# A decoder layer in fp32: squares and residual of the output projection added by transfers, and the MLP's first group in another order

## The chip, the cores and the metric

The kernel runs on 1 core of a Trainium2 chip. The metric is the time of one execution in device microseconds. Before the change the median of three runs is 2737.82 us (2735.27 to 2740.61).

## The reference, cut to what matters

One decoder layer over 2048 tokens of width 1024. Two groups of token-mixer heads (a gated delta rule and HGRN2) make `mix`; the lines that the change bears on come after them:

```python
mix_out = jnp.einsum('btc,cd->btd', mix, w_out[i])          # 1024 x 1024
h = h + rms_norm(mix_out, post_mix_norm[i])

u = jnp.einsum('btd,df->btf', rms_norm(h, pre_mlp_norm[i]), w_mlp_up[i])   # 1024 -> 4096
y = jnp.einsum('btf,fd->btd', jnp.square(jax.nn.relu(u)), w_mlp_down[i])
h = h + rms_norm(y, post_mlp_norm[i])
...
gate = jax.nn.sigmoid(jnp.einsum('btd,de->bte', h, w_ple_gate[i]))
return h + e * gate
```

`rms_norm` needs the sum of squares of a token over all 1024 columns, and the second norm (of `h`, before the MLP) needs it again for the sum of the first norm's result and the residual.

## The kernel before, in words

**Arithmetic.** Every large matmul is made of three: an fp32 operand is split into a high half, copied by ScalarE (ACT), and a low half, the difference, made by VectorE (DVE) (`split`, L164 and L165), and high x high, high x low and low x high are summed in PSUM. TensorE (PE) thus waits for a block until ACT and DVE have both treated it.

**Stages.** The mixers run until about 1105 us, then the output projection (tiles `mmo`, to 1316), the MLP's up projection in Strassen's form (tiles `u`: seven products of half-size blocks for each group of columns), the down projection (`d`) and the gate (`mmg`).

**Output projection.** Tokens lie in four quarters q of 512, output columns in eight blocks d of 128, and the loop runs over 32 tiles j = 8q + d; a tile is 24 matmuls (8 blocks of the inner dimension by 3). Tiles 0 and 1 are made early, among the mixers. For tile j, `stage_out` starts the load of 512 KB of weights three tiles ahead (`raw_out`, 2 buffers), `ready_out` splits it two tiles ahead into `w_out` (3 buffers). In quarter 0 the split weights are also kept in DRAM, and quarter 3 reloads them whole, 1 MB a tile (`w_out24` to `w_out31`, L185). ACT copies the finished bank to `yo` and squares it (`squares`): the first square of a quarter goes into `acc_o`, the others into a scratch tile `sq_o`, which DVE adds to `acc_o` (L228).

**Norm and residual.** At the end of a quarter `rstd_steps` makes 1/rms from `acc_o` with two matmuls against ones and some work on ACT and DVE. For quarters 0 and 1 `residual` follows: for each of eight tiles it loads `xo` from the input (SP's queue, L1139), scales `yo` (DVE, L1188), adds `xo` (DVE, L1189), squares the sum into `sq_h`/`acc_h`, and stores it to `h1d` (L1185, L1195). `early_operands` loads parts of `h1d` back (`be`), scales and splits them into the operands `t11`, `t21` of the first MLP group. Quarters 2 and 3 are only stored (`yod`) and treated later.

**What sets the order.** PE's order is written by hand and kept. Every eighth matmul calls `tick()`, which advances generators that `later(gen, offsets)` has put at given ticks; `OUT_STEPS` gives the ticks of the norm and the residual. DVE, ACT, GpSimd (POOL) and SyncE (SP, which issues nearly all transfers) each run their instructions in the order that results from it, and an instruction that waits holds what stands behind it on its engine.

**Start of the MLP.** In the last tiles of the projection the four blocks of the first up weights are loaded into two tiles `u_raw` and split. Blocks that are sums or differences ("3", "1", "2", "4") are made by DVE in place. The first group is made `together`: its last five products share their passes over the inner dimension:

```python
seven = (("11", "11"), ("12", "21"), ("2", "2"), ("3", "3"), ("22", "4"), ("1", "1"), ("4", "22"))
...
for k in range(KD // 2):
    for ps, (w, m) in zip(sums, rest):
        product(ps, columns(x[w])[k : k + 1], t[m][k : k + 1], k == 0, k == KD // 2 - 1)
```

`up_weights(0, 1)` makes the blocks `wu` of the second group: its first step loads the blocks `a` (L1381), and the rest (splits and sums) runs when the first group has been issued and the projection's buffers are closed, since the blocks' pool `bp` lies in their space.

Of the kernel before, what the change touches and what calls it, by code (L numbers as in the profile page):

```python
# [10 lines left out]
F32 = mybir.dt.float32  # L11
# [35 lines left out]
OUT_STEPS = (1, 5) + tuple(range(7, 15)) + (15, 25)  # L47
# [41 lines left out]
def trunk(ctx, tc, x, xT, pT, vecs, w_in, w_ab, gdn_a_log, gdn_dt_bias, w_out, w_up, w_down,  # L89
# [129 lines left out]

    def squares(acc, src, k, name, eng=V):  # L220

        if acc is None:
            acc = st.tile([P, QT], F32, tag="acc", name=f"acc_{name}", bufs=3)
            S.activation(acc, src, AF.Square)
        else:
            sq = st.tile([P, QT], F32, tag="sq", name=f"sq_{name}_{k}", bufs=1)
            S.activation(sq, src, AF.Square)  # L227
            eng.tensor_tensor(acc, acc, sq, ALU.add)  # L228
        return acc
# [967 lines left out]

    def normed(q, ys, acc, skip, gain, dst, name, sums=None, pool=None):

        rd = []  # L1200
        yield from rstd_steps(acc, 1.0 / D, EPS, f"{name}{q}", rd.append, pool)
        total = yield from residual(q, lambda d: ys[d], rd[0], skip, gain, dst, name, sums)
# [20 lines left out]
    def run(gen):  # L1223
        for _ in gen:
            pass
# [85 lines left out]

    for j, (q, d) in enumerate(order):
# [36 lines left out]
        acc = squares(acc, ps, d, f"o{q}")  # L1349
# [7 lines left out]
    b2 = two_blocks(("1", s1), None)  # L1357
    V.tensor_tensor(a11, s1, a11, ALU.subtract)
# [6 lines left out]
    bp = []  # L1365

    def block(name):

        return bp[0].tile([P, 2, KD // 2, P], F32R, tag="blk", name=name)
# [69 lines left out]
    def up(half, g, x, between, together=False):  # L1439
# [12 lines left out]
        for i, (w, m) in enumerate(seven):  # L1452
# [52 lines left out]
    def down_pair(half, j):  # L1505
# [5 lines left out]
        a = bp[0].tile([P, 2, QT], F32R, tag="blk", name=f"da_{half}_{j}")  # L1511
# [7 lines left out]
        b = bp[0].tile([P, 2, QT], F32R, tag="blk", name=f"db_{half}_{j}")  # L1519
# [160 lines left out]
    def embedded(q, d, rsb):  # L1680

        t = bp[0].tile([P, 2, QT], F32, tag="blk", name=f"eg{q}_{d}")
# [100 lines left out]
```

## Time and profile before

| | |
|---|---|
| median of 3 runs | 2737.82 us (2735.27 to 2740.61) |
| profiled execution, its own time | 2733.95 us |
| its span | 2732.0 us, granted PE clock 0.993 |
| PE busy | 2661.9 us, 97% |
| DVE, ACT, POOL busy | 2047.2 (75%), 1469.8 (54%), 101.5 (4%) us |
| output projection, quarters 0 to 3 | about 1133 to 1316 us |
| first MLP group | 1316 to about 1360 us |

How to read it: PE runs nearly without a break, so the time is its work plus its idle time and the matmuls that run at less than the full rate. A share of 75% for DVE is a mean over the stages; in the stretch from 1200 to 1260 us it is busy for 52.24 of 60 us.

### The profile page before, as it was taken

To read this page: it belongs to the slowest core of one execution; us is meant where nothing else is said; L and a number is where in the kernel's file an instruction comes from. 1 tells how busy PE (TensorE), PEld (TensorE's weight loads), DVE (VectorE), ACT (ScalarE), POOL (GpSimd) and SP (SyncE) were. 2 spreads that over 40 slices of the span, in tenths; PEclk is the share of its full clock that TensorE was granted. 3 is DMA by queue.
4 is the path that set the end of the run, shared out by engine and by line. 5 is a ranking of instruction groups with operands and counts; after the bars stand their busy time and mean duration, and the time that the engine had idled before them with its cause. 6 is when DMAs were issued, how large, how long until landed. Compare 5 with 4: busy or idle time off the path is not lost.

```text
span 2732.0 us, 38440 instructions
## 1 busy us (share of the span) xinstructions
PE 2661.9 (97%) x12745; PEld 2217.0 (81%) x12745; DVE 2047.2 (75%) x4244; ACT 1469.8 (54%) x2944; POOL 101.5 (4%) x104
## 2 busy tenths in 40 slices
PE   7999999999999999999899999999999999999999
PEld 5788888888888887877788888888888888888887
DVE  6788877787778777577889867767787765567776
ACT  6665554465446445576555645555454455465422
POOL 0000000000000000000000000001000000001000
PEclk9999999999999999999999999999999999999999
DMA  7777777667666665787466547667564446687663
GB/s 247 264 262 229 243 251 251 220 224 256 203 212 220 214 216 163 267 295 239 150 225 224 189 149 260 205 208 241 170 204 145 152 171 208 191 256 246 215 211 133
DMA packets 268741, 589.23 MB, mean 216 GB/s; under 512 B 55658, under 2 KB 60232, under 8 KB 249344
## 3 DMA queue, kind: packets, MB, share of 16 engines
q1 hardware_dynamic: 268544, 586.79, 64.7%
q8 instruction: 101, 1.65, 0.3%
q14 instruction: 96, 0.79, 0.1%
HBM read 419.75 MB, written 166.92 MB: 215 GB/s over the span
## 4 chain that ended last, share of the span: by engine, by line
PE 51%; DVE 3%; DMA 3%; issue 2%; ACT 2%; POOL 1%; SPq 0%; POOLq 0%; DVEq 0%; ACTq 0%
PE u L1119 22%; PE d L1119 21%; PE mmg L1119 6%; PE mmo L1119 1%; POOL acc_y L228 1%; DMA raw_out<-in_w_out_dram 1%; DMA xo<-in_xT_dram 0%; DMA b<-h1d 0%; DMA mixT<-mixd 0%; DVE t L165 0%; DMA rd_g<-m_g 0%; DVE w_out L165 0%; DMA raw_pT<-in_pT_dram 0%; DVE yo L1189 0%; ACT L1156 0%
## 5 line engine op out<-in xcount | busy, mean ns | idle before, releaser
L1048 PE MATMUL mm<-xt,w 128*128 128x512 f32 x3072 | 783.8, 400 | 1.7 <-ACT zt_zg L553 1.5
L1048 PEld LDWEIGHTS mm<-xt,w 128*128 128x128 f32 x3072 | 553.4, 189 | 102.2 <-ACT zt_zg L553 1.9
L1119 PE MATMUL d<-db,da 128*128 128x512 f32 x2688 | 610.5, 389 | 0.2 <-DVE db L218 0.2
L1119 PE MATMUL u<-t,wu 128*128 128x512 f32 x2604 | 593.2, 390 | 3.4 <-ACT wu L164 3.4
L1119 PEld LDWEIGHTS d<-db,da 128*128 128x128 f32 x2688 | 504.6, 188 | 105.5 <-DVE db L218 0.5
L1119 PEld LDWEIGHTS u<-t,wu 128*128 128x128 f32 x2604 | 489.6, 188 | 106.4 <-ACT wu L164 4.2
L218 DVE TENSOR_TENSOR db<-db 128x512 fp32r<-128x512 f32 x224 | 160.9, 718 | 68.8 <-ACT db L217 68.3
L1448 DVE TENSOR_TENSOR u<-u,u 128x512 f32<-128x512 f32 x224 | 150.5, 683 | 63.0 <-PE u L1119 61.2
L1119 PE MATMUL mmo<-mixT,w_out 128*128 128x512 f32 x720 | 170.5, 398 | 10.9 <-DVE w_out L165 6.3
L217 ACT ACTIVATE db<-db 128x512 fp32r<-128x512 f32 x224 | 140.9, 629 | 73.5 <-DMA db<-hid 69.2
L1119 PE MATMUL mmg<-h2T,wg 128*128 128x512 f32 (+1 forms) x792 | 174.7, 383 | 0.0
L1119 PEld LDWEIGHTS mmo<-mixT,w_out 128*128 128x128 f32 x720 | 138.1, 193 | 42.3 <-DVE w_out L165 8.0
L1489 ACT ACTIVATE u<-u 128x512 f32<-128x512 f32 x128 | 80.9, 632 | 167.5 <-DVE u L1448 167.0
L1119 PEld LDWEIGHTS mmg<-h2T,wg 128*128 128x128 f32 x792 | 145.5, 188 | 29.1
L165 DVE TENSOR_TENSOR da<-da 128x512 fp32r<-128x512 f32 x128 | 92.3, 721 | 83.0 <-ACT da L164 82.8
L164 ACT ACTIVATE da<-da 128x512 fp32r<-128x512 f32 x128 | 80.5, 629 | 128.1 <-DMA da<-sumd 110.4
L164 ACT ACTIVATE wu<-a 128x512 fp32r<-128x512 f32 x124 | 73.9, 622 | 50.1 <-DMA a<-in_w_up_dram 48.5
L674 DVE TENSOR_TENSOR pr_g<-xs_g,sys_g 128x16 f32<-128x16 f32 (+14 forms) x240 | 94.3, 393 | 5.6
L228 POOL TENSOR_TENSOR acc_y<-acc_y,sq_y 128x512 f32<-128x512 f32 x28 | 38.8, 1386 | 1371.6 <-ACT sq_y L227 1332.5
L165 DVE TENSOR_TENSOR wu<-a,wu 128x512 fp32r<-128x512 f32 x124 | 84.8, 688 | 3.3 <-ACT wu L164 3.2
L1490 ACT ACTIVATE u<-u 128x512 f32<-128x512 f32 x128 | 80.7, 631 | 3.7
L165 DVE TENSOR_TENSOR da<-dr,da 128x512 fp32r<-128x512 f32 x96 | 66.3, 691 | 18.2 <-ACT da L164 16.1
(383 smaller groups left out, 3792.0 us busy)
## 6 DMA issues: line engine op xcount, KB each, us to landing
w<-cache_in SPq DMA_DIRECT2D x96, 1024.0 KB
db<-hid SPq DMA_DIRECT2D x224, 256.0 KB
cache_in<-w SPq DMA_DIRECT2D x32, 1024.0 KB
hid<-u SPq DMA_DIRECT2D x128, 256.0 KB
da<-sumd SPq DMA_DIRECT2D x128, 256.0 KB
a<-in_w_up_dram SPq DMA_DIRECT2D x124, 256.0 KB
hid<-ht SPq DMA_DIRECT2D x96, 256.0 KB
dr<-in_w_down_dram SPq DMA_DIRECT2D x96, 256.0 KB
```

Of the source, the lines that this page charges most:

```text
L164: S.activation(t[:, 0], raw, AF.Copy)
L165: eng.tensor_tensor(t[:, 1], raw, t[:, 0], ALU.subtract)
L217: S.activation(t[:, 0], plain(t), AF.Copy)
L218: V.tensor_tensor(t[:, 1], plain(t), t[:, 0], ALU.subtract)
L228: eng.tensor_tensor(acc, acc, sq, ALU.add)
L674: V.tensor_tensor(pr[:, :, :, 0:i], xs[:, None, :, 0:i].broadcast_to([P, 2, GC, i]), sys[:, 0:i, i : i + 2].rearrange("p j two -> p two j" ...
L1048: PE.matmul(ps, *terms[i], start=i == 0, stop=i == nt - 1)
L1119: PE.matmul(ps, a, b, start=start, stop=stop)
L1448: V.tensor_tensor(c[new], c[old], ps, ALU.add)
L1489: S.activation(c[k], c[k], AF.Relu)
L1490: S.activation(c[k], c[k], AF.Square)
```

## The change

Six edits, of which the first four concern the output projection.

1. `squares` can add by a transfer: for tiles 1 to 6 of every quarter the sum `acc_o += sq_o` becomes a transfer issued by POOL that adds to its target (`accum_op`). Tile 7 stays with DVE.
2. `residual_by_dma` takes the place of `residual` for quarters 0 and 1: DVE scales `yo`, and a transfer from the input in DRAM adds the residual to it. The loads `xo` go. Squares and stores run three steps later, and `OUT_STEPS` has three more steps.
3. During the projection the scratch tile of a square alternates between the buffers "late" (2) and "sq" (1).
4. `early_operands` takes every second tick instead of each.
5. In the first MLP group the differences for "2" and "4" are made before the split of "3", and the five shared products run as "3" and "22" first, then "2", "1", "4".
6. Two of ten block buffers get a pool of their own (`b2`) ahead of `bp`, so that the second group's first blocks can be split during the first group's third and fourth product.

```diff
-OUT_STEPS = (1, 5) + tuple(range(7, 15)) + (15, 25)
+OUT_STEPS = (1, 5) + tuple(range(7, 18)) + (18, 26)
...
+            turns[0] += 1
+            if pair[0] and turns[0] % 2:
+                sq = st.tile([P, QT], F32, tag="late", name=f"sq_{name}_{k}")
+            else:
+                sq = st.tile([P, QT], F32, tag="sq", name=f"sq_{name}_{k}", bufs=1)
             S.activation(sq, src, AF.Square)
-            eng.tensor_tensor(acc, acc, sq, ALU.add)
+            if eng is None:
+                G.dma_start(acc, sq, accum_op=ALU.add)
+            else:
+                eng.tensor_tensor(acc, acc, sq, ALU.add)
...
+    def residual_by_dma(q, ys, rsb, skip, gain, dst, name, sums):
+
+        total, lag = None, 3
+        for d in range(KD + lag):
+            yield
+            if d < KD:
+                V.scalar_tensor_tensor(ys[d], ys[d], col(gain + d), rsb, ALU.mult, ALU.mult)
+                G.dma_start(ys[d], skip(d), accum_op=ALU.add)
+            if d >= lag:
+                total = squares(total, ys[d - lag], d - lag, f"{sums}{q}")
+                nc.sync.dma_start(dst[d - lag], ys[d - lag])
...
+            V.tensor_tensor(a11, s1, a11, ALU.subtract)
+            V.tensor_tensor(s4, s4, a11, ALU.subtract)
             u_block("3", b22, a21)
         if (q, d) == (2, 1):
             early = early_operands()
-            later(early, range(KD))
+            later(early, range(0, 2 * KD, 2))
...
-        acc = squares(acc, ps, d, f"o{q}")
+        acc = squares(acc, ps, d, f"o{q}", V if d + 1 == KD else None)
...
-    b2 = two_blocks(("1", s1), None)
-    V.tensor_tensor(a11, s1, a11, ALU.subtract)
-    u_block("2", b2, a11)
-    V.tensor_tensor(s4, s4, a11, ALU.subtract)
+    u_block("2", two_blocks(("1", s1), None), a11)
     u_block("4", wp.tile([P, 2, KD // 2, P], F32R, tag="raw", name="w_u4", bufs=2), s4)
     run(prep)
+    pair[0] = False
...
+    bp, blocks = [ctx.enter_context(tc.tile_pool(name="b2", bufs=2, reuse_waits="tile"))], [0]
...
+                for them in ((1, 2), (0, 3, 4)):
+                    for k in range(KD // 2):
+                        for r in them:
+                            w, m = rest[r]
+                            product(sums[r], columns(x[w])[k : k + 1], t[m][k : k + 1], k == 0, k == KD // 2 - 1)
...
-    up(0, 0, x, {}, True)
+    up(0, 0, x, {2: [gen], 3: [gen]}, True)
     wctx.close()
-    bp.append(ctx.enter_context(tc.tile_pool(name="bp", bufs=10, side="right", reuse_waits="tile")))
+    bp.append(ctx.enter_context(tc.tile_pool(name="bp", bufs=8, side="right", reuse_waits="tile")))
```

**How the order moves.** The names carry a running number; a first number after `yo`, `h1d`, `xo` is the quarter, the next the tile. First DVE's row in quarter 2, around the low half of `w_out22`, in the kernel before:

```order
L1189 TENSOR_TENSOR yo1_2_12656<-yo1_2_12656,xo1_2_13093 128x512
L1247 SCALAR_TENSOR_TENSOR be_3_13134<-be_3_13134,cols_87,rn0_12951 128x512
L1188 SCALAR_TENSOR_TENSOR yo1_3_12719<-yo1_3_12719,cols_87,r_o1_13021 128x512
L228 TENSOR_TENSOR acc_h1_13076<-acc_h1_13076,sq_h1_2_13131 128x512
L165 TENSOR_TENSOR t11_0_3_13137<-be_3_13134,t11_0_3_13137 128x512
L1189 TENSOR_TENSOR yo1_3_12719<-yo1_3_12719,xo1_3_13127 128x512
L1247 SCALAR_TENSOR_TENSOR be_7_13156<-be_7_13156,cols_87,rn0_12951 128x512
L1188 SCALAR_TENSOR_TENSOR yo1_4_12784<-yo1_4_12784,cols_87,r_o1_13021 128x512
L228 TENSOR_TENSOR acc_h1_13076<-acc_h1_13076,sq_h1_3_13153 128x512
L165 TENSOR_TENSOR t21_0_3_13159<-be_7_13156,t21_0_3_13159 128x512
L1189 TENSOR_TENSOR yo1_4_12784<-yo1_4_12784,xo1_4_13149 128x512
L165 TENSOR_TENSOR w_out22_13192<-raw_out22_13123,w_out22_13192 128x1024
```

The scaling (L1188), the residual add (L1189) and the add of squares (L228) of quarter 1 stand interleaved with the operands `be` and `t` of the MLP, ahead of the split. After the change, the same stretch beginning right behind the low half of `w_out21`:

```order
L1213 SCALAR_TENSOR_TENSOR yo1_3_12696<-yo1_3_12696,cols_87,r_o1_12999 128x512
L1213 SCALAR_TENSOR_TENSOR yo1_4_12757<-yo1_4_12757,cols_87,r_o1_12999 128x512
L1273 SCALAR_TENSOR_TENSOR be_2_13115<-be_2_13115,cols_87,rn0_12946 128x512
L1213 SCALAR_TENSOR_TENSOR yo1_5_12812<-yo1_5_12812,cols_87,r_o1_12999 128x512
L237 TENSOR_TENSOR acc_h1_13098<-acc_h1_13098,sq_h1_1_13111 128x512
L165 TENSOR_TENSOR t11_0_2_13118<-be_2_13115,t11_0_2_13118 128x512
L1213 SCALAR_TENSOR_TENSOR yo1_6_12862<-yo1_6_12862,cols_87,r_o1_12999 128x512
L165 TENSOR_TENSOR w_out22_13135<-raw_out22_13077,w_out22_13135 128x1024
L237 TENSOR_TENSOR acc_h1_13098<-acc_h1_13098,sq_h1_2_13143 128x512
L1273 SCALAR_TENSOR_TENSOR be_6_13161<-be_6_13161,cols_87,rn0_12946 128x512
L237 TENSOR_TENSOR acc_h1_13098<-acc_h1_13098,sq_h1_3_13157 128x512
L1213 SCALAR_TENSOR_TENSOR yo1_7_12909<-yo1_7_12909,cols_87,r_o1_12999 128x512
```

The scalings (now L1213) run ahead of the adds of squares (L237), the residual adds are gone, and the low half of `w_out22` stands eight rows behind that of `w_out21`. The add of `sq_h1_3` stands ahead of the scaling of `yo1_7`.

SP's queue before quarter 3, in the kernel before (L185 is the reload of 1 MB):

```order
L1185 DMA h1d1_2_139<-yo1_2_12656 128x512
L1139 DMA xo1_4_13149<-in_xT_dram 128x512
L1185 DMA h1d1_3_140<-yo1_3_12719 128x512
L1139 DMA xo1_5_13171<-in_xT_dram 128x512
L185 DMA w_out24_13288<-cache_out0_11786 128x2048
L1185 DMA h1d1_4_141<-yo1_4_12784 128x512
L1139 DMA xo1_6_13199<-in_xT_dram 128x512
L1352 DMA yod2_5_12206<-yo2_5_13282 128x512
L1326 DMA u_raw0_13515<-in_w_up_dram 128x512
L1185 DMA h1d1_5_142<-yo1_5_12831 128x512
```

and after:

```order
L1217 DMA h1d1_5_142<-yo1_5_12812 128x512
L1291 DMA b2_0_0_13372<-h1d1_0_137 128x512
L1381 DMA yod2_4_12205<-yo2_4_13189 128x512
L1217 DMA h1d1_6_143<-yo1_6_12862 128x512
L1291 DMA b3_0_0_13375<-h1d1_4_141 128x512
L1353 DMA u_raw0_13483<-in_w_up_dram 128x512
L1217 DMA h1d1_7_144<-yo1_7_12909 128x512
L1353 DMA u_raw1_13484<-in_w_up_dram 128x512
L185 DMA w_out24_13253<-cache_out0_11786 128x2048
L1381 DMA yod2_5_12206<-yo2_5_13247 128x512
L1353 DMA u_raw0_13483<-in_w_up_dram 128x512
```

The loads `xo` are gone, and the reload `w_out24`, which stood between the stores of `h1d1_3` and `h1d1_4`, stands behind the store of `h1d1_7` and two loads of up weights.

PE's row in the first MLP group, in the kernel before, behind the second product:

```order
L1119 MATMUL u2_0_0_13828<-t2_0_0_13466,w_u1_13772 128x512 x3
L1119 MATMUL u3_0_0_13829<-t3_0_0_13441,w_u22_13721 128x512 x3
L1119 MATMUL u22_0_0_13830<-t4_0_0_13479,w_u22_13721 128x512 x3
L1119 MATMUL u1_0_0_13831<-t1_0_0_13444,w_u1_13772 128x512 x3
L1119 MATMUL u4_0_0_13832<-t22_0_0_13482,w_u4_13779 128x512 x3
L1119 MATMUL u2_0_0_13828<-t2_0_1_13551,w_u1_13772 128x512
L1150 MATMUL nrm_o3_13849<-hl_o3_13802,ones_94 128x512
L1151 MATMUL nrm_o3_13849<-hl_o3_13802,ones_94 128x512
L1119 MATMUL u2_0_0_13828<-t2_0_1_13551,w_u1_13772 128x512 x2
```

and after:

```order
L1128 MATMUL u3_0_0_13806<-t3_0_0_13409,w_u22_13689 128x512 x3
L1128 MATMUL u22_0_0_13807<-t4_0_0_13447,w_u22_13689 128x512 x3
L1128 MATMUL u3_0_0_13806<-t3_0_1_13503,w_u22_13689 128x512 x3
L1128 MATMUL u22_0_0_13807<-t4_0_1_13541,w_u22_13689 128x512 x3
L1128 MATMUL u3_0_0_13806<-t3_0_2_13589,w_u22_13689 128x512 x3
L1128 MATMUL u22_0_0_13807<-t4_0_2_13618,w_u22_13689 128x512
L1159 MATMUL nrm_o3_13826<-hl_o3_13773,ones_94 128x512
L1160 MATMUL nrm_o3_13826<-hl_o3_13773,ones_94 128x512
L1128 MATMUL u22_0_0_13807<-t4_0_2_13618,w_u22_13689 128x512 x2
L1128 MATMUL u3_0_0_13806<-t3_0_3_13669,w_u22_13689 128x512 x3
L1128 MATMUL u22_0_0_13807<-t4_0_3_13714,w_u22_13689 128x512 x3
L1128 MATMUL u2_0_0_13805<-t2_0_0_13434,w_u1_13742 128x512 x3
```

Before, each pass takes one step of "2" (`w_u1`'s other half), "3", "22", "1" and "4" in turn; now "3" and "22" have all their passes ahead of the first step of "2", with the two matmuls of the norm `nrm_o3` among them.

More of the change, by code (lines that the diff above doesn't have):

```diff
@@ L218, in split_in_place @@
         V.tensor_tensor(t[:, 1], plain(t), t[:, 0], ALU.subtract)
+    pair, turns = [False], [0]
     def squares(acc, src, k, name, eng=V):
@@ L1196, in residual @@
         return total
+    def residual_by_dma(q, ys, rsb, skip, gain, dst, name, sums):
[8 more added lines that the diff above has]
+                nc.sync.dma_start(dst[d - lag], ys[d - lag])
+        yield
+        return total
     def normed(q, ys, acc, skip, gain, dst, name, sums=None, pool=None):
@@ L1201, in normed @@
         yield from rstd_steps(acc, 1.0 / D, EPS, f"{name}{q}", rd.append, pool)
-        total = yield from residual(q, lambda d: ys[d], rd[0], skip, gain, dst, name, sums)
+        if name == "o":
+            total = yield from residual_by_dma(q, ys, rd[0], skip, gain, dst, name, sums)
+        else:
+            total = yield from residual(q, lambda d: ys[d], rd[0], skip, gain, dst, name, sums)
         if sums is not None:
@@ L1310, in two_blocks @@
         return halves[1]
+    pair[0] = True
     for j, (q, d) in enumerate(order):
@@ L1510, in down_pair @@
         g = j % NG
-        a = bp[0].tile([P, 2, QT], F32R, tag="blk", name=f"da_{half}_{j}")
+        a = turn_block([P, 2, QT], F32R, f"da_{half}_{j}")
         if len(wn) == 2:
@@ L1518, in down_pair @@
             nc.sync.dma_start(raw, tile[:, at * QT : (at + 1) * QT])
-        b = bp[0].tile([P, 2, QT], F32R, tag="blk", name=f"db_{half}_{j}")
+        b = turn_block([P, 2, QT], F32R, f"db_{half}_{j}")
         nc.sync.dma_start(plain(b), hidd[half, hn, g])
@@ L1680, in embedded @@
     def embedded(q, d, rsb):
-        t = bp[0].tile([P, 2, QT], F32, tag="blk", name=f"eg{q}_{d}")
+        t = turn_block([P, 2, QT], F32, f"eg{q}_{d}")
         nc.sync.dma_start(t[:, 0], ed[q][d])
```

10 lines of the change are left out of this document (4 added, 6 removed).

## The prediction

> **What bounds the kernel now.** I read the busy shares first, then the waits of TensorE (PE) between 1105 and 1360 us, then PE's timeline for the same stretch, then the windows of the output projection.
>
> ```profile
> PE 2661.9 (97%) x12745; PEld 2217.0 (81%) x12745; DVE 2047.2 (75%) x4244; ACT 1469.8 (54%) x2944; POOL 101.5 (4%) x104
> PE mmo L1119 <- DVE w_out L165: 6.3, 4, 3.1
> PE u L1119 <- ACT w_u L164: 4.1, 1, 4.1
> PE u L1119 <- ACT wu L164: 3.4, 2, 2.5
> PE mmo L1119 <- ACT sq_o L227: 2.4, 1, 2.4
> PE mmo L1119 <- ACT w_out L164: 2.2, 1, 2.2
> ```
>
> PE is busy for 2661.9 of 2732.0 us: 70 us of idle time is all that any reordering can win, and a change elsewhere counts only by what PE waits for. The five rows (total us, count, longest) name the waits of the stages that the change edits: the output projection (mmo) and the first MLP group (u). The timeline shows where they are, and a second loss behind them.
>
> ```profile
> 1168.30 0.73 PE L1119 MATMUL mmo<-mixT,w_out 128*128 128x512 f32 x2 [2.20 <-ACT w_out L164]
> 1169.56 8.91 PE L1119 MATMUL mmo<-mixT,w_out 128*128 128x512 f32 x38 [0.53 <-DVE w_out L165]
> ...
> 1215.80 3.48 PE L1119 MATMUL mmo<-mixT,w_out 128*128 128x512 f32 x8 [2.43 <-ACT sq_o L227]
> ...
> 1240.87 5.73 PE L1119 MATMUL mmo<-mixT,w_out 128*128 128x512 f32 x24 [0.25 <-DVE w_out L165]
> 1248.93 7.32 PE L1119 MATMUL mmo<-mixT,w_out 128*128 128x512 f32 x24 [2.33 <-DVE w_out L165]
> 1259.40 14.13 PE L1119 MATMUL mmo<-mixT,w_out 128*128 128x512 f32 x54 [3.15 <-DVE w_out L165]
> ...
> 1281.52 34.62 PE L1119 MATMUL mmo<-mixT,w_out 128*128 128x512 f32 x152
> 1315.98 5.60 PE L1119 MATMUL u<-t,w_u 128*128 128x512 f32 x24
> 1325.70 6.75 PE L1119 MATMUL u<-t,w_u 128*128 128x512 f32 x16 [4.12 <-ACT w_u L164]
> ...
> 1343.71 6.10 PE L1119 MATMUL u<-t,wu 128*128 128x512 f32 x24 [0.82 <-ACT wu L164]
> 1352.36 7.82 PE L1119 MATMUL u<-t,wu 128*128 128x512 f32 x27 [2.54 <-ACT wu L164]
> ```
>
> Columns: start, length, count, the wait before it in brackets. The row of 152 gives the full rate: 34.62/152 = 0.2278 us a matmul, so one output tile (24 matmuls) takes 5.47 us. Rows behind a wait are slower than that: 8 took 3.48 (1.66 too long), 24 took 7.32 (1.85), 54 took 14.13 (1.83), 16 took 6.75 (3.11), 27 took 7.82 (1.67). So a wait costs itself and then some lost clock:
>
> - token quarter 0: 2.20 + 0.53 = 2.7
> - quarters 1 and 2: waits 2.43 + 0.25 + 2.33 + 3.15 = 8.2, slow matmuls 1.66 + 0.26 + 1.85 + 1.83 = 5.6, together 13.8
> - start of the MLP: waits 4.12 + 0.82 + 2.54 = 7.5, slow matmuls 3.11 + 1.67 = 4.8, together 12.3
>
> The sum, 28.8 us, is the most the change can win here.
>
> ```profile
> 1133.00:1200.00 67.00, 64.28 (x281) 52.61 (x282) 38.95 (x54) 42.22 (x67) 2.02 (x2) 1.00 0.86 297
> 1200.00:1260.00 60.00, 51.84 (x211) 41.46 (x211) 52.24 (x79) 39.38 (x59) 0.00 (x0) 0.94 0.71 231
> 1316.00:1360.00 44.00, 36.43 (x138) 28.15 (x137) 32.73 (x53) 22.84 (x38) 0.00 (x0) 0.88 0.36 118
> ```
>
> Columns: stretch, length, busy time of PE, its weight loads, VectorE (DVE), ScalarE (ACT) and GpSimd (POOL), granted clock, share of the DMA engines, GB/s. The granted clock is 0.94 and 0.88 in the stretches with waits and 1.00 in the first. By the Trainium skill ("TensorE: Matmul & The Clock Gate", Part 1) the clock falls only after an idle window of some 3.4 us; here 24 matmuls lost 1.85 us after a wait of 2.33 us, so the measurement decides, and by the page only the 4.12 wait would carry a clock price (3.1 us of the 10.4).
>
> The two middle stages differ in kind. From 1200 to 1260 DVE is busy for 52.24 of 60 us, and what PE waits for is DVE's low half of a weight tile. From 1316 to 1360 DVE is at 32.73 of 44: there the order of the program is late, not an engine.
>
> **What comes off DVE.** The change takes 24 of the 28 adds of squares and all 16 residual adds off DVE.
>
> ```profile
> L228 DVE TENSOR_TENSOR acc_o<-acc_o,sq_o x28: 682/686/693, 1134.1 to 1323.1; 128x512 f32<-128x512 f32 x28
> L1189 DVE TENSOR_TENSOR yo<-yo,xo x16: 681/684/693, 1190.0 to 1268.1; 128x512 f32<-128x512 f32 x16
> 1241.99 0.75 DVE L1188 SCALAR_TENSOR_TENSOR yo<-yo,cols,r_o 128x512 f32<-128x512 f32 x1
> 1247.65 1.22 DVE L165 TENSOR_TENSOR w_out<-raw_out,w_out 128x1024 fp32r<-128x1024 f32 x1
> 1258.13 1.22 DVE L165 TENSOR_TENSOR w_out<-raw_out,w_out 128x1024 fp32r<-128x1024 f32 x1
> ```
>
> 24 × 0.686 + 16 × 0.684 = 16.5 + 10.9 = 27.4 us of DVE work, all between 1134 and 1323. It only counts where PE waits for DVE. Between the scaling at 1241.99 and the low halves of w_out21 (1247.65) and w_out22 (1258.13) stand seven adds that go (two of squares, five of residuals; counted in DVE's timeline from the first of these rows to the last), three of them ahead of w_out21. In the new order w_out21's half stands behind three scalings and no add, so it would be done at about 1244.5, before PE finishes tile 20 at 1246.6. The three waits of 0.25, 2.33 and 3.15 go, and the wait of 2.43 (a PSUM bank held by a late square) loses its cause with the second scratch buffer. Upper bound of this term: −13.8.
>
> **What stands in its place.** Each residual tile is now a chain: scaling on DVE, an accumulating transfer issued by POOL, its landing, then the square on ACT and the store to h1d on SP. SP is in order, and the first 1 MB weight reload of quarter 3 (w_out24), which stood between the stores of h1d1_3 and h1d1_4, now stands behind all eight, h1d1_7 the last. And DVE's scaling of yo1_7 stands behind the add of sq_h1_3, which needs yo1_3's landing: two transfers in a row before the reload can be issued. No row of before has a transfer issued by POOL or one that adds; the nearest rows are loads of the same 256 KB (the first three) and of 512 KB:
>
> ```profile
> 1191.13 4.04 DMA xo<-in_xT_dram
> 1196.40 4.69 DMA xo<-in_xT_dram
> 1153.24 4.81 DMA mixT<-mixd
> 1159.71 7.45 DMA raw_out<-in_w_out_dram
> 1255.99 0.40 SPq L185 DMA_DIRECT2D w_out<-cache_out  x1
> ```
>
> I take 4.7 us for a transfer with its issue, bounded below by 4.04 and above by 2 × 4.81 = 9.6 (it reads the target before it writes it: an estimate, twice the row). With 4.7: yo1_3 scaled at 1245.4, landed 1250.1; square, add and the scaling of yo1_7 behind it, about 0.6 + 0.7 + 0.75, done 1252.2; landed 1256.9; then h1d1_7, u_raw1 and the reload issue at about 1258.5 instead of 1255.99. The reload lands between 4.8 and 7.45 us later, at 1263.3 to 1266. PE reached tile 24 at about 1259.40 + 48 matmuls = 1271.6; without its 13.8 us of loss it comes at 1257.8, and at 1260 to 1261 with what quarter 0 costs below. So a new wait of about 4 us with 2 us of slow clock behind it: −13.8 + 6 = −8 (from −13.8 at a transfer of 4.0 us and a fast reload to 0 at 7.5 us; each microsecond more delays tile 24 by two).
>
> By the Trainium skill ("DMA: Bandwidth & Descriptors", section "Anatomy of one DMA — SWDGE (gpsimd) path") such a transfer takes 2.0 us plus its bytes at 436 GB/s: 2.6 us for 256 KB, an estimate, by which the reload would be issued some 4 us sooner and this term be −12; nothing in before shows it.
>
> **Quarter 0 pays.** There DVE was not short (38.95 of 67 us), so the six adds removed win nothing, and three things are added.
>
> ```profile
> 1133.49 0.61 ACT L227 ACTIVATE sq_o<-mmo 128x512 f32<-128x512 f32 x1
> 1152.67 1.06 ACT L164 ACTIVATE w_out<-raw_out 128x1024 fp32r<-128x1024 f32 x1 [1.77 <-DMA raw_out<-in_w_out_dram]
> 1141.16 0.43 SPq L571 DMA_DIRECT2D mixd<-og_h  x1
> 1148.89 1.01 POOL L160 TENSOR_TENSOR m_g<-m_g,mhalf 128x4 f32<-128x4 f32 x1 [8.14 <-DVE m_g L274]
> q1 hardware_dynamic: 7831, 19.86, 85.4%
> ```
>
> First, the square of tile 1 (1133.49) now takes a "late" buffer, which is held until the store of og_h, issued at 1141.16, has landed; in order on ACT, the high half of w_out6 (1152.67) and PE's tile copies stand behind the squares. Second, the transfers that add into acc_o form a chain, each waiting for the one before; at 4.7 us they fit into a tile's 5.47 by 0.8. Third, POOL's m_g (1148.89), which the mixer's last normalisation and so the late weight load at 1159.71 wait for, stands behind such a transfer in POOL's order. The queue row is for 1133 to 1200: 19.86 MB with the engines busy at 85.4%. A wait of one more microsecond at two places with slow clock behind: +3.5, from 0 (all hidden under PE's 24-matmul tiles) to +10 (the engines' free 15% of 67 us filled).
>
> **Start of the MLP.** PE's first eight products' operands stand ready; at 1321.6 (1315.98 + 5.60) it wants block "2", made last.
>
> ```profile
> 1317.21 3.20 SPq L1381 DMA_DIRECT2D a<-in_w_up_dram  x4
> 1320.20 0.63 ACT L164 ACTIVATE w_u<-u_raw 128x512 fp32r<-128x512 f32 x1
> 1321.29 0.69 DVE L165 TENSOR_TENSOR w_u<-u_raw,w_u 128x512 fp32r<-128x512 f32 x1
> 1324.30 0.69 DVE L1358 TENSOR_TENSOR u_raw<-u_raw,u_raw 128x512 f32<-128x512 f32 x1
> 1325.02 0.63 ACT L164 ACTIVATE w_u<-u_raw 128x512 fp32r<-128x512 f32 x1 [0.57 <-DVE u_raw L1358]
> ```
>
> The subtraction at 1324.30 is moved ahead of the split whose low half is at 1321.29 (done 1321.98), and PE now goes through "3" and "22" first: 24 products and two of a norm, 26 × 0.2278 = 5.9 us, so block "2" is wanted at about 1327.5 where ACT began it at 1325.02 even before. The wait of 4.12 and its clock go; what remains is at most 0.4 for "3", plus the subtractions now ahead of it, 2 × 0.69. The waits of 0.82 and 2.54 for the next group's blocks go because these are split during the third and fourth product; their loads, issued from 1317.21, are there 7 us before. What moves onto ACT ahead of the norm (two splits, 2 × 0.63) I charge with 1.3: −12.3 + 1.3 = −11, from −12.3 to −5 (the norm or "4" late).
>
> **Sum.** −11 − 8 + 3.5 = −15.5; I round to −15. The profiled execution took 2733.95 (span 2732.0), 3.87 below the median 2737.82 of the three runs (2735.27 to 2740.61). So 2719 against the profiled run and **2723** on the median. A measurement here tells some 0.2% (5.5 us) from no change. The likeliest case's own range is 2710 to 2733, from its terms' ends taken together only in part.
>
> **Rivals.**
>
> - *The transfers fill the DMA engines.* For it: 85.4% in quarter 0, 0.71 from 1200 to 1260. 40 transfers of 256 KB that read and write their target are added and 16 loads dropped; quarter 0 gets the full +10 and quarters 1 and 2 give back half their gain: −11 − 6 + 12 = −5 or so, 2733. Against: the load of quarters 1 and 2 barely grows. The Trainium skill ("DMA: Bandwidth & Descriptors", section "Issuing engines are not separate DMA queues") says that queues of all engines share the same 16 DMA engines; the rows of before show one queue only, so they can't show it. Chance 0.14.
> - *Slower: the chain of transfers sets the pace.* An accumulating transfer takes longer than a tile. From 5.47 us on, the chain of acc_o holds the three scratch buffers, then ACT's squares, then PE's banks; and at 8 to 9 us the reload of w_out24 comes 2 × 4 us later than above. Quarter 0's six and quarters 1 and 2's twelve chained transfers at 3 us too much each, half of it hidden: 18 × 1.5 = +27, less 11 for the MLP: +16, 2754. For it: the 7.45 row, a chain without slack, POOL's one order for both kinds of transfer. Against: the rows of 4.0 to 4.8. It decides from about 7.5 us a transfer. Chance 0.20.
> - *The first group gains little.* Blocks are reordered, but ACT takes the new splits in a worse place (norm first, "1" and "2" behind them), or the loads behind 1317.21 land later than the third product: −5 instead of −11, 2729 to 2731. Chance 0.10.
> - The forecast: 0.56.
>
> Faster by over 0.2% (below 2732): the forecast nearly whole, 0.52, half of the third rival and a third of the first, 0.10: 0.62. Within 0.2%: 0.15. Slower: the second rival and the tail of the first, 0.23. The range takes in the whole bound of the gain less 2 below (2737.82 − 28.8 + 2 = 2711) and half of the slower rival above: 2711 to 2748.
>
> **What would show it.** Right: no wait of PE for w_out's low half between 1240 and 1262, the x16 row after u's first products at 0.228 a matmul, a wait for w_out24 of some 4 us at the start of quarter 3, small new waits in quarter 0. Wrong: accumulating transfers of over 5.5 us from issue to landing, PE waiting for ACT's sq_o or copies in quarter 0, or a wait of the first group for "3" or the norm of more than 2 us. If w_out24 doesn't wait at all, the transfers are near 2.6 us and the gain is nearer 20.

## The result: slower by 0.9%, and the profile after

| | before | changed |
|---|---|---|
| median | 2739.22 us (2735.27 to 2742.16, 4 runs) | 2765.59 us (2763.93 to 2768.14, 4 runs) |
| profiled execution's span | 2732.0 us | 2763.8 us |

The ratio is 1.0094 with a 95% interval of 1.0081 to 1.0106: slower, where faster was forecast, and above the range. The runs below were timed in groups, each with executions of the kernel before beside it (their medians lie between 2734.5 and 2739.2 us), so runs of different groups are compared by their ratios. I read the changed kernel's waits of PE first (1105 to 1420 us; total, count, longest), then PE's timeline.

```profile
PE mmo L1128 <- ACT w_out L164: 21.0, 5, 5.9
PE mmo L1128 <- DMA w_out<-cache_out: 6.5, 2, 3.5
PE u L1128 <- ACT w_u L164: 3.0, 1, 3.0
PE mmo L1128 <- DVE mixT L218: 2.6, 1, 2.6
PE nrm_o L1159 <- ACT hl_o L164: 2.1, 1, 2.1
```

```profile
1160.12 13.96 PE L1128 MATMUL mmo<-mixT,w_out 128*128 128x512 f32 x48 [3.49 <-ACT w_out L164]
1179.94 7.01 PE L1128 MATMUL mmo<-mixT,w_out 128*128 128x512 f32 x16 [5.86 <-ACT w_out L164]
1189.55 7.31 PE L1128 MATMUL mmo<-mixT,w_out 128*128 128x512 f32 x24 [2.60 <-DVE mixT L218]
...
1236.37 6.16 PE L1128 MATMUL mmo<-mixT,w_out 128*128 128x512 f32 x16 [4.60 <-ACT w_out L164]
...
1276.39 8.41 PE L1128 MATMUL mmo<-mixT,w_out 128*128 128x512 f32 x24 [3.92 <-ACT w_out L164]
1287.92 0.74 PE L1128 MATMUL mmo<-mixT,w_out 128*128 128x512 f32 x2 [3.12 <-ACT w_out L164]
...
1300.35 3.96 PE L1128 MATMUL mmo<-mixT,w_out 128*128 128x512 f32 x16 [3.00 <-DMA w_out<-cache_out]
...
1336.52 18.06 PE L1128 MATMUL mmo<-mixT,w_out 128*128 128x512 f32 x72 [3.49 <-DMA w_out<-cache_out]
1354.41 5.60 PE L1128 MATMUL u<-t,w_u 128*128 128x512 f32 x24
1363.06 0.77 PE L1128 MATMUL u<-t,w_u 128*128 128x512 f32 x2 [3.04 <-ACT w_u L164]
```

PE's waits for DVE's low halves are all but gone, as intended. In their place it waits for ACT's high halves, 21.0 us in five waits: in quarter 0 (1160.12), ahead of tile 8 (1179.94), ahead of tile 16 (1236.37) and at tiles 22 and 23 (1276.39, 1287.92). Quarter 3, whose weights are reloaded whole, has no such wait. Tile starts, counted in PE's timeline at 24 matmuls a tile, give the stages, so a wait ahead of a quarter's first tile counts to the quarter before it. "Rest" is from the first product of the MLP to the end of the span; the rows below "changed" are those of the experiments.

| kernel | q0 (tiles 2 to 7) | q1 | q2 | q3 | rest | median, us | ratio to before (95%) |
|---|---|---|---|---|---|---|---|
| before | 35.0 | 47.5 | 55.6 | 44.5 | 1416.0 | 2734.5 to 2739.2 | |
| changed | 45.3 | 56.4 | 64.0 | 54.1 | 1409.4 | 2765.6 | 1.0081 to 1.0106 |
| e1 MLP edits only | 35.5 | 47.4 | 55.9 | 44.5 | 1406.4 | 2725.9 | 0.9953 to 0.9978 |
| e2 + squares by transfer | 43.8 | 52.3 | 63.3 | 54.6 | 1407.6 | 2754.2 | 1.0059 to 1.0084 |
| e3 + residual by transfer | 34.9 | 47.5 | 59.1 | 46.4 | 1407.8 | 2730.9 | 0.9971 to 0.9989 |
| e4 changed, copies in place of adds | 40.7 | 50.2 | 54.8 | 49.3 | 1406.5 | 2738.1 | 0.9998 to 1.0016 |
| e5 e1 + scratch tiles | 35.7 | 49.0 | 59.1 | 44.6 | 1405.7 | 2725.6 | 0.9955 to 0.9979 |
| e6 e5 + two chains in q0 | 40.7 | 47.5 | 58.2 | 44.7 | 1405.0 | 2728.3 | 0.9970 to 0.9989 |
| e7 e5 + squares of q1, q2 on POOL | 35.1 | 46.8 | 60.1 | 44.7 | 1405.8 | 2728.3 | 0.9970 to 0.9987 |
| e8 e3 with lag 5 | 35.1 | 46.6 | 56.9 | 46.3 | 1406.0 | 2727.9 | 0.9963 to 0.9983 |
| e9 e8 + 2 reloads on POOL | 35.1 | 45.1 | 50.5 | 51.6 | 1404.0 | 2722.1 | 0.9941 to 0.9970 |
| e10 e1 again | 35.0 | 48.7 | 55.9 | 44.5 | 1405.2 | 2724.9 | 0.9945 to 0.9974 |
| e11 e9 + all reloads on POOL | 34.5 | 45.1 | 51.4 | 49.2 | 1414.2 | 2733.3 | 0.9974 to 0.9991 |

The changed kernel's four quarters lost 10.3, 8.9, 8.4 and 9.6 us, the MLP won 6.6; with 1.4 before tile 2 that is the 31.8 us between the spans. Why ACT is late shows in quarter 0. First POOL's row, then ACT's, then the landing times of the transfers (tile views of acc_o and of yo, 1133 to 1400) and the software queue's row for 1133 to 1370 (packets, MB, share of 16 engines).

```profile
1147.18 1.05 POOL L235 DMA_DIRECT2D acc_o<-sq_o  x1 [4.63 <-ACT sq_o L233]
1155.15 0.88 POOL L235 DMA_DIRECT2D acc_o<-sq_o  x1 [6.92 <-DMA acc_o<-sq_o]
...
1159.04 0.92 POOL L235 DMA_DIRECT2D acc_o<-sq_o  x1 [1.95 <-DMA acc_o<-sq_o]
1169.08 0.86 POOL L235 DMA_DIRECT2D acc_o<-sq_o  x1 [9.12 <-DMA acc_o<-sq_o]
1177.79 0.86 POOL L235 DMA_DIRECT2D acc_o<-sq_o  x1 [7.85 <-DMA acc_o<-sq_o]
1181.82 0.86 POOL L235 DMA_DIRECT2D acc_o<-sq_o  x1 [3.17 <-DMA acc_o<-sq_o]
```

```profile
1154.93 0.60 ACT L233 ACTIVATE sq_o<-mmo 128x512 f32<-128x512 f32 x1 [6.25 <-DMA acc_o<-sq_o]
...
1168.62 0.60 ACT L233 ACTIVATE sq_o<-mmo 128x512 f32<-128x512 f32 x1 [2.97 <-DMA acc_o<-sq_o]
...
1177.34 0.60 ACT L233 ACTIVATE sq_o<-mmo 128x512 f32<-128x512 f32 x1 [7.11 <-DMA acc_o<-sq_o]
...
1178.83 1.06 ACT L164 ACTIVATE w_out<-raw_out 128x1024 fp32r<-128x1024 f32 x1
```

```profile
DMA to landing us min/median/max: 3.3/6.1/10.2
DMA to landing us min/median/max: 6.3/9.2/14.4
q0 software_dynamic: 5760, 10.49, 25.4%
```

From the first to the last issue the six transfers stand (1181.82 − 1147.18)/5 = 6.9 us apart, each issued when the one before has landed; a tile of PE takes 5.47. The scratch tiles run out, ACT waits 7.11 us to write a square, and the high half of the weights that PE waits 5.86 us for (1179.94) stands three instructions behind that square, at 1178.83. It is the same ahead of tile 16 and at tile 23, with squares held by the chain, and at tile 22, where ACT stood 6.28 us at a square that needed the residual's transfer:

```profile
1234.78 0.60 ACT L233 ACTIVATE sq_o<-mmo 128x512 f32<-128x512 f32 x1 [1.19 <-DMA acc_o<-sq_o]
1235.27 1.05 ACT L164 ACTIVATE w_out<-raw_out 128x1024 fp32r<-128x1024 f32 x1
...
1271.09 0.63 ACT L226 ACTIVATE acc_h<-yo 128x512 f32<-128x512 f32 x1 [6.28 <-DMA yo<-in_xT_dram]
...
1286.33 0.60 ACT L233 ACTIVATE sq_o<-mmo 128x512 f32<-128x512 f32 x1 [3.52 <-DMA acc_o<-sq_o]
1286.82 1.05 ACT L164 ACTIVATE w_out<-raw_out 128x1024 fp32r<-128x1024 f32 x1
```

### The profile page after: what moved, and what is told of

The parts are those of the page before. It is cut to its first block, busy times and chain, and to the rows that moved or that the text cites. A ratio compares the mean times of both kernels' runs of the same rounds, so it can differ in the third digit from the quotient of the medians.

```text
span 2763.8 us, 38502 instructions
## 1 busy us (share of the span) xinstructions
PE 2673.3 (97%) x12745; PEld 2222.8 (80%) x12745; DVE 2022.8 (73%) x4204; ACT 1467.4 (53%) x2944; POOL 137.2 (5%) x144
## 3 DMA queue, kind: packets, MB, share of 16 engines
q0 software_dynamic: 5760, 10.49, 2.2%
## 4 chain that ended last, share of the span: by engine, by line
PE 48%; DVE 1%; DMA 1%; ACT 1%; POOL 1%; issue 0%; SPq 0%; POOLq 0%; ACTq 0%; DVEq 0%
PE u L1128 21%; PE d L1128 20%; PE mmg L1128 6%; POOL acc_y L237 1%; ACT sq_y L233 0%; DMA dr<-in_w_down_dram 0%; DMA db<-hid 0%; DMA acc_o<-sq_o 0%; DVE t L165 0%; DMA da<-sumd 0%; DMA eg<-ed 0%; DVE wu L165 0%; DVE hl_y L165 0%; DVE w_u L165 0%; ACT da L164 0%
## 5 line engine op out<-in xcount | busy, mean ns | idle before, releaser
L1128 PE MATMUL mmo<-mixT,w_out 128*128 128x512 f32 x720 | 184.5, 418 | 30.8 <-ACT w_out L164 21.0
L1128 PEld LDWEIGHTS mmo<-mixT,w_out 128*128 128x128 f32 x720 | 145.6, 204 | 68.8 <-ACT w_out L164 23.1
L237 POOL TENSOR_TENSOR acc_y<-acc_y,sq_y 128x512 f32<-128x512 f32 x28 | 38.8, 1387 | 1192.3 <-ACT sq_y L233 1191.6
L165 DVE TENSOR_TENSOR wu<-a,wu 128x512 fp32r<-128x512 f32 x124 | 85.8, 694 | 11.0 <-ACT wu L164 10.8
```

The source lines that it names most:

```text
L165: eng.tensor_tensor(t[:, 1], raw, t[:, 0], ALU.subtract)
L1128: PE.matmul(ps, a, b, start=start, stop=stop)
```

## The experiments

**e1, the MLP edits alone.** Squares and residual as before, one scratch tile, ticks and operand steps as before.

```diff
-OUT_STEPS = (1, 5) + tuple(range(7, 18)) + (18, 26)
+OUT_STEPS = (1, 5) + tuple(range(7, 15)) + (15, 25)
-        if name == "o":
+        if False:
-    pair[0] = True
+    pair[0] = False
-            later(early, range(0, 2 * KD, 2))
+            later(early, range(KD))
-        acc = squares(acc, ps, d, f"o{q}", V if d + 1 == KD else None)
+        acc = squares(acc, ps, d, f"o{q}")
```

> Only the edits to the MLP's start are left (differences first, products 3 and 22 ahead, block buffers split 2 and 8, second group's blocks split early); squares and residual are added by DVE as in the kernel before, with its one scratch tile and its ticks. In the changed kernel the time from the first product of the MLP to the end fell by 6.6 us (1416.0 to 1409.4), with one wait of 3.0 left for a block whose split stood behind a square on ACT. Theory 1 (the MLP edits are sound, the transfers spoilt a part): faster than before by 9 to 12 us, and no wait over 1 us for w_u or wu. Theory 2 (the reordered group gains no more than that by itself): faster by about 6 us. If it is not faster, the 6.6 us came from something that the transfers freed.

2725.93 us (5 runs), 9 us below before. PE's timeline has no wait for w_u or wu any more, and the window of the MLP's start (before: PE busy for 36.43 of 44 us, clock 0.88) reads:

```profile
1316.00:1360.00 44.00, 43.27 (x190) 35.24 (x189) 39.91 (x66) 28.20 (x48) 0.00 (x0) 1.00 0.42 137
```

Theory 1 holds: the MLP edits are worth 9.6 us in the profile, and the changed kernel got 6.6 of them. Its wait of 3.04 at 1363.06 is for a block whose subtraction DVE made only at 1361.65; DVE had waited 4.62 us for splits that stood on ACT behind a square of quarter 3, which a landing held for 4.79 us.

**e2, squares by transfers, residual on DVE.** From the changed kernel:

```diff
-OUT_STEPS = (1, 5) + tuple(range(7, 18)) + (18, 26)
+OUT_STEPS = (1, 5) + tuple(range(7, 15)) + (15, 25)
-        if name == "o":
+        if False:
-            later(early, range(0, 2 * KD, 2))
+            later(early, range(KD))
```

> The changed kernel with the residual added by DVE again (with the loads, ticks and operand steps of before); squares still added by transfers, scratch tiles alternate, MLP edits kept. Theory 1 (the chain of squares' transfers, one waiting for the other through acc_o, with ACT's squares and weight halves behind it, is the larger cost): quarter 0 loses its 9.6 us again and quarter 3 most of its 9.5, so slower than before by 8 to 18 us. Theory 2 (the residual's transfers, 9.2 us to landing, are the larger cost and lengthen the others by crowding): transfers of squares land in about 3.5 to 5 us, and the time is within 5 us of before.

2754.24 us, 28.3 above e1. (The alternating scratch tiles, which e2 also has, are worth nothing by themselves: e5.) All four quarters lose (8.3, 4.9, 7.4, 10.1 us against e1). Theory 1, with a price somewhat above its upper end; the landings (3.3, 5.2, 9.3 for least, middle, most) stay long with no residual transfer beside them.

**e3, residual by transfers, squares on DVE.**

```diff
-        acc = squares(acc, ps, d, f"o{q}", V if d + 1 == KD else None)
+        acc = squares(acc, ps, d, f"o{q}")
```

> The changed kernel with all squares added by DVE; the residual still added by transfers in quarters 0 and 1, MLP edits and scratch tiles kept. Theory 1 (the squares' transfers are the larger cost): quarters 0 and 3 as in before, quarters 1 and 2 within 8 us of before either way, the MLP 9 to 12 us shorter: 0 to 15 us faster than before. Theory 2 (the residual's are): quarters 1 and 2 lose most of what the changed kernel lost there (18 us), so slower than before by 5 us or more, with PE waiting for w_out behind squares of h on ACT.

2730.89 us (11 runs), 4 below before and 5 above e1: theory 1 again. The residual's transfers take 5.5 us of adds (8 of 0.684) for each quarter off DVE and still win nothing: quarter 2 is 3.2 us longer than in e1. Its landings are 3.8, 6.7 and 10.7 us. SP's row shows the held reload that the prediction described, w_out24 issued 10.6 us later than before:

```profile
1266.58 0.43 SPq L185 DMA_DIRECT2D w_out<-cache_out  x1
```

**e4, the same transfers without the add.** The sums of squares and the residual are thus left out of the result.

```diff
-                G.dma_start(acc, sq, accum_op=ALU.add)
+                G.dma_start(acc, sq)
...
-                G.dma_start(ys[d], skip(d), accum_op=ALU.add)
+                G.dma_start(ys[d], skip(d))
```

> The changed kernel with all 40 transfers made plain copies over their targets, in the same queue, places and waits: the sums of squares and the residual are left out of the result. Theory 1 (adding at the target is what makes a transfer slow): transfers of 256 KB land in 3 to 5 us, quarters 0 and 3 lose at most 3 us each, and the time is 10 us or more below the changed kernel's 2765. Theory 2 (the queue that GpSimd fills, its issue and the crowding of the 16 engines make them slow): landings of 5 to 9 us as with the add, time within 4 us of the changed kernel.

2738.13 us (11 runs): some 24 below the changed kernel by the ratios. The same bytes took half the engines' time (the software queue's row for 1133 to 1370, where the changed kernel has 5760 packets and 25.4%, then the landings of acc_o and yo):

```profile
q0 software_dynamic: 3200, 10.49, 12.4%
DMA to landing us min/median/max: 2.2/4.7/8.1
DMA to landing us min/median/max: 4.5/6.5/7.1
```

Adding doubles what a transfer costs the engines (25.4 against 12.4%) and lengthens its landing by 1.4 to 2.7 us. Theory 1 holds for the larger part, not for all: quarters 0 and 3 still lose 5.7 and 4.8 us, more than the 3 it allowed, and the residual's copies land in 6.5 us, not in 3 to 5. A chain of plain copies is still 12 us worse than DVE's adds in e1.

**e5, the scratch tiles alone.** e1 with `pair[0] = True`.

> The MLP edits and the alternating scratch tiles, no transfer that adds: the kernel of e1 with squares taking the two 'late' buffers and the one 'sq' buffer in turn. Theory 1 (the scratch tile held PE's bank): the wait of 2.3 us for a square at the start of quarter 2 goes with its slow matmuls, 2 to 4 us below e1 (2726), about 2723. Theory 2 (the 'late' buffers are also those of the residual loads xo, so a square now waits for a load and the loads for a square): within 1.5 us of e1 or above it.

2725.59 us, e1's time: theory 2. The wait for PE's bank (2.3 us in e1) is gone from the profile, but PE's waits for w_out's low halves rose from 6.7 to 9.2.

**e6, two chains in quarter 0.**

```diff
...
+        if q > 0:
+            acc = squares(acc, ps, d, f"o{q}")
+        elif d < 2:
+            chains = (chains if d else []) + [squares(None, ps, d, f"o{q}_{d}", home=odd if d else None)]
+        else:
+            squares(chains[d % 2], ps, d, f"o{q}", V if d + 1 == KD else None)
...
```

One add on DVE joins the two sums at the end, and five transfers are left of six.

> The kernel of e5 with the squares of quarter 0 added by transfers, but into two sums (even and odd tiles, joined by one add on DVE), so that a transfer waits for the one before the last. Five transfers instead of six; quarters 1 to 3 on DVE. Theory 1 (the loss in quarter 0 is the chain: each transfer's landing added to the next one's wait, with ACT's squares and weight halves behind it): tile 8 starts within 2 us of where it starts in e5 and the time is within 2 us of e5. Theory 2 (the transfers crowd the 16 engines, whatever their order): tile 8 is late by 4 us or more, as in e2 (1174.5 against 1170.2 in e1), and the time is 4 to 9 us above e5.

Quarter 0 takes 40.7 us, 5.0 above e5 where one chain cost 8.3 in e2; the median (2728.28) is only 2.7 above e5, with overlapping intervals. Tile 8 starts 1.8 us after e5's, as theory 1 said, but only because tile 2 had started 3.2 us sooner; e7's tile 2 started as early (1130.5), and its quarter took 35.1. So neither theory alone: two chains give back some 3 us, and what is left looks like crowding. PE's wait of 5.5 us at tile 8 is for a weight half that waited for its load, not for a square; that load, issued at 1160.74, took 8.7 us, where e5's (1161.23) took 6.4. The engines are at 0.93 from 1130 to 1172, where e5 has 0.87 (third row), and move no more bytes a second:

```profile
1169.45 1.06 ACT L164 ACTIVATE w_out<-raw_out 128x1024 fp32r<-128x1024 f32 x1 [3.76 <-DMA raw_out<-in_w_out_dram]
1130.00:1172.00 42.00, 35.02 (x148) 27.19 (x147) 10.62 (x14) 16.39 (x26) 6.60 (x7) 0.98 0.93 297
1133.00:1170.00 37.00, 33.94 (x147) 27.09 (x146) 14.57 (x20) 16.22 (x26) 2.02 (x2) 1.00 0.87 296
```

**e7, squares of quarters 1 and 2 added by GpSimd's instructions.** From e5:

```diff
+        acc = squares(acc, ps, d, f"o{q}", G if q in (1, 2) and 0 < d < KD - 1 else V)
```

> The kernel of e5 with 12 of the adds of squares (tiles 1 to 6 of quarters 1 and 2) made by GpSimd as instructions, not as transfers, so that DVE loses 12 x 0.69 = 8.2 us of work where PE waits for it. Theory 1 (DVE's row is what PE waits for in quarter 2, and an add takes about 1.4 us on GpSimd, less than a tile): the waits for the low halves of w_out in quarter 2 (5.7 us in e1) shrink by a third to a half with the slow matmuls behind them, 2 to 6 us below e5. Theory 2 (an add on GpSimd slows DVE's own instructions, or its later end holds the scratch tile and ACT): DVE's 512-column adds take more than 0.72 us in the mean, and the time is that of e5 or above it.

2728.25 us (11 runs), not below e5: theory 1 fails. GpSimd's adds took longer than hoped, with least, middle and most in ns:

```profile
L237 POOL TENSOR_TENSOR acc_o<-acc_o,sq_o x12: 1290/1606/2122, 1186.6 to 1273.6; 128x512 f32<-128x512 f32 x12
L237 DVE TENSOR_TENSOR acc_o<-acc_o,sq_o x11: 679/692/695, 1143.1 to 1296.2; 128x512 f32<-128x512 f32 x11
```

DVE's own adds did not slow (692 ns), so theory 2's first reason fails; that later squares held the scratch tile is likely from a wait of 1.7 us for sq_o that e5 does not have, but not shown further.

**e8, residual by transfers with squares and stores five steps later.** From e3:

```diff
-OUT_STEPS = (1, 5) + tuple(range(7, 18)) + (18, 26)
+OUT_STEPS = (1, 5) + tuple(range(7, 20)) + (20, 26)
-        total, lag = None, 3
+        total, lag = None, 5
```

> The kernel of e3 (residual by transfers, squares on DVE) with squares and stores five steps behind the transfer instead of three, and the steps that this needs in the ticks (7 to 19, 20, 26). Theory 1 (ACT stands at a square that waits for a landing, 6.7 us in the middle and up to 10.7, with the high halves of w_out behind it): PE's waits for w_out in quarters 1 and 2 (9.2 us in e3, the reload apart) fall to 5 or less, and the time is 3 to 6 us below e3 (2731). Theory 2 (the transfers' own length on the crowded engines delays the loads of w_out): waits stay within 2 us of e3's and the time within 2.5 us.

2727.87 us, 3.0 below e3's median, but 1.9 by the ratios, and the intervals overlap: the time decides nothing. PE's waits for w_out's halves, all quarters, fall from 10.4 to 5.0 us, as theory 1 said: ACT had stood at squares whose landing was not there. Nearly as much went into the reload, which SP issues at 1265.55 and PE now waits 7.39 us for (e3: 2.30).

**e9, two reloads issued by POOL.** From e8:

```diff
-        nc.sync.dma_start(w.bitcast(F32).rearrange("p h k n -> p (h k n)"), cached[key])
+        (G if name in ("out24", "out25") else nc.sync).dma_start(w.bitcast(F32).rearrange("p h k n -> p (h k n)"), cached[key])
```

> The kernel of e8 with the first two reloads of quarter 3 (w_out24, w_out25) issued by GpSimd, behind its last residual transfer, instead of by SP behind the stores of h1d1. Theory 1 (SP's row held the reload: e8 issued it at 1265.6, PE waited 7.4 us for it): the reload is issued by about 1258, PE's wait for it falls below 2 us, and the time is 4 to 8 us below e8 (2728), so 2720 to 2724, below e1 too. Theory 2 (the reload was late because the engines were full, or its buffer came free late): issued about 2 us sooner at most or landing in over 8 us, wait over 5 us, time within 2.5 us of e8.

```profile
1252.02 0.81 POOL L185 DMA_DIRECT2D w_out<-cache_out  x1
1263.40 3.94 PE L1128 MATMUL mmo<-mixT,w_out 128*128 128x512 f32 x16 [0.98 <-DMA w_out<-cache_out]
1297.21 3.20 PE L1128 MATMUL mmo<-mixT,w_out 128*128 128x512 f32 x7 [3.75 <-DMA w_out<-cache_out]
```

2722.09 us, 5.8 below e8's median and 4.9 by the ratios, whose intervals just overlap; the reload's early issue and short wait (0.98) are theory 1's. Quarter 2 falls to 50.5 us, 5.1 below the kernel before, and quarter 3 gives it back: 51.6, with 3.75 us of waiting for w_out29.

**e10, e1 again beside e9.**

> The kernel of e1 once more, on the same chip and beside the same runs as e9, for the comparison of the two: 2724 to 2728 by both theories. If theory 1 of e9 holds, e9 is below it by 2 us or more.

2724.92 us (ratio to before 0.9945 to 0.9974). e9 is 2.8 below, but the intervals overlap: whether the residual by transfers is worth anything over DVE's adds, even with lag and reloads mended, stays open.

**e11, all eight reloads on POOL.** e9 with the names out24 to out31.

> The kernel of e9 with all eight reloads of quarter 3 issued by GpSimd. In e9 quarter 2 became 5 us shorter than in the kernel before but quarter 3 7 us longer (51.6 against 44.5): PE waited 3.8 us for w_out29, issued by SP at 1289.0 behind a store of yod that waited for its copy. Theory 1 (the same holding of SP's row, one step later): quarter 3 falls to 45 to 48 us and the time to 2716 to 2720. Theory 2 (the engines are full there, or the copies are late by themselves): quarter 3 stays above 49 us and the time within 2.5 us of e9 (2722).

2733.28 us (12 runs, ratio 0.9974 to 0.9991), 11 above e9's median and some 8 by the ratios: neither theory. PE waits for no reload after tile 24, and quarter 3 falls only to 49.2; the MLP takes 10.2 us longer, with a wait for a block made late. SP's stores of yod (19.69 us for four) stood ahead of the loads of the MLP's operands, which is the likely cause, not tested:

```profile
PE u L1128 <- ACT w_u L164: 6.2, 1, 6.2
PE mmo L1128 <- DMA w_out<-cache_out: 2.8, 1, 2.8
1275.76 19.69 SPq L1381 DMA_DIRECT2D yod<-yo  x4
```

## Why the prediction was wrong

- **The start of the MLP, −11: right.** It measured −9.6 alone (e1; −10.8 in e10) and −6.6 in the changed kernel, where the landings took 3 back. The reason given, block "2" no longer wanted first, is what PE's timeline shows.
- **DVE's 27 us off, the waits for low halves gone: right and without effect.** From 1200 to 1260 DVE is busy for 37.16 us instead of 52.24, and of the waits for low halves of w_out one of 0.52 us is left in the projection. But the waits for ACT that took their place are longer.

```profile
1133.00:1200.00 67.00, 54.85 (x206) 42.58 (x205) 21.46 (x28) 28.27 (x45) 7.51 (x8) 0.87 0.78 248
1200.00:1260.00 60.00, 55.36 (x235) 44.89 (x234) 37.16 (x53) 40.44 (x62) 12.31 (x14) 0.94 0.92 255
```

- **The step that failed: 4.7 us for a transfer, taken from loads, and the chain of squares charged to quarter 0 alone.** Adding transfers landed in 6.1 us (squares) and 9.2 us (residual) in the middle, 10.2 and 14.4 at most. The upper bound of 9.6 held both middles, and I took the value near the lower rows, although the range's own turning points (5.47 for a tile, 7.5 for the stage) lay between. But the price is only half of it. The sum put the chain of squares at nothing in quarters 1 to 3, where by itself it cost 4.9, 7.4 and 10.1 us (e2 against e1). With plain copies, which landed in 4.7 and 6.5 us, the four quarters still took 195.0 us against 182.6 before, where the sum had them 4.5 us shorter (e4).
- **Adding against copying.** The Trainium skill ("Collectives: The Full Stack", section "The bandwidth ceiling: the fold count and why AG ≠ RS ≠ AR") says that a ReduceScatter reaches half the rate of an AllGather because its add needs two source reads. For the engines' time the trace agrees, 25.4 against 12.4% for the same 10.49 MB; the landings did not double (6.1 against 4.7 us, 9.2 against 6.5), and that the second read is the cause is not shown here.
- **Quarters 1 and 2, −8: measured +17.3** (8.9 + 8.4). The mechanism named, w_out24 behind the stores of h1d1, was there (issued at 1291.44 in the changed kernel, a wait of 3.00 at tile 24) but was the lesser part. ACT, not SP, was the queue that hurt: squares stand there that need a landed transfer, with the weights' high halves behind them. I had named ACT's row only for quarter 0. And a chain reaches past its quarter: DVE's add for tile 7 of quarter 0 waited 5.32 us for the last landing, with splits of mixT behind it on DVE and ACT, and PE waited 2.60 us for one in quarter 1 (1189.55).
- **Quarter 0, +3.5: measured +10.3**, just above the upper end of 10, by the second of its three reasons, the chain: both of PE's waits for it (3.49 and 5.86) end with a half that stood behind a square held by the chain.
- **Quarter 3, not priced: measured +9.6.** It has no splits of w_out, and its own six squares are not what PE waits for there. What it paid for is the end of quarter 2's chain:

```profile
1303.96 0.86 POOL L235 DMA_DIRECT2D acc_o<-sq_o  x1 [8.84 <-ACT sq_o L233]
1311.67 0.63 ACT L164 ACTIVATE hl_o<-acc_o 128x512 fp32r<-128x512 f32 x1 [8.19 <-DVE acc_o L237]
1312.36 0.78 PE L1159 MATMUL nrm_o<-hl_o,ones 128*128 128x512 f32 x1 [2.15 <-ACT hl_o L164]
...
1325.31 0.58 ACT L1377 ACTIVATE yo<-mmo 128x512 f32<-128x512 f32 x1
1325.92 0.32 SPq L1381 DMA_DIRECT2D yod<-yo  x1
1327.31 0.36 SPq L185 DMA_DIRECT2D w_out<-cache_out  x1
```

The last transfer of quarter 2 goes out only at 1303.96 (the row names ACT's square, but that was written by 1295.97; what was left to wait for is the landing of the transfer issued at 1294.25). So the norm is late: ACT waits 8.19 us and PE 2.15 for it. A copy to yo then stands on ACT behind that norm, its store on SP behind the copy, and the reload of w_out29 behind the store; w_out29 is what PE waits 3.49 us for at 1336.52. In e2 the same quarter pays in the same way: a square of quarter 2 holds ACT, and the norm's matmul waits for what stands behind it.

```profile
1297.75 0.60 ACT L233 ACTIVATE sq_o<-mmo 128x512 f32<-128x512 f32 x1 [5.22 <-DMA acc_o<-sq_o]
1298.92 0.79 PE L1159 MATMUL nrm_h<-hl_h,ones 128*128 128x512 f32 x1 [6.72 <-ACT hl_h L164]
```

The quarter's own chain was felt in the MLP instead (the wait of 3.04 named under e1). This is the omission that mattered: the cost was argued for the quarter whose trace had a visible neighbour (mixer and late load) and not carried to the others with the same edit, nor past a quarter's end.

- **The rivals.** "The chain of transfers sets the pace" is what happened, at +31 us in quarters 0 to 3 from e1 to e2 (8.3 + 4.9 + 7.4 + 10.1 = 30.7 in the profiles) where I had +27 with half hidden. "The transfers fill the engines" has some support as a second part (e6). Neither excludes the other. A transfer of a square landed in 2.2 us at least as a copy, in 3.3 at least as an add and in 10.2 at most; how much of that spread is crowding stays open.

How the loss divides, by the ratios to before: the MLP edits −10 us (e1), squares by transfers +29 (e2 against e1), residual by transfers +4 (e3 against e1). That leaves 2 of the 35 us between e1 and the changed kernel for both kinds together, which is within the intervals. Within the squares' 29, the runs give a share to the add itself and to the chain, not a clean split.

## What to carry to other kernels

A transfer that adds is not a free adder: price it by its landing under the load of that stage, and multiply by the number of transfers that wait for one another. Before moving an add from an engine into a transfer, list what waits for the landing on every in-order engine; a 0.7 us instruction on a busy engine was here cheaper than a 6 us landing that ACT stood in front of. And apply a cost found in one stage to each stage with the same edit, and to what stands behind the end of its chain in the stage after.

## What the runs showed of the hardware

- A transfer of 256 KB that adds took twice the engine time of a copy (25.4 against 12.4% of the same stretch) in more packets (5760 against 3200), and 3.3 us at least to land, against 2.2. By the Trainium skill ("DMA: Bandwidth & Descriptors", section "Anatomy of one DMA — SWDGE (gpsimd) path") it would be 2.6 us (an estimate); a copy's least is below that, an add's is above, and in the middle both are far above (4.7 and 6.1), so the measurement decides.
- GpSimd needed 0.86 to 1.05 us to issue an adding transfer of a square and 0.87 to 1.93 for one of the residual (256 KB each, changed kernel), 0.54 to 0.72 for the same as copies (e4), and 0.54 to 0.81 for a copy of 1 MB (e9, e11).
